# A hybrid decoder layer in float32: the MLP's down projection done one product at a time in all eight PSUM banks

## The chip, the cores and the metric

The kernel runs on one core of one Trainium2 chip. A core has a matrix engine (TensorE, PE in the profile), a vector engine (VectorE, DVE), an activation engine (ScalarE, ACT), a general engine (GpSimd, POOL) and a queue engine (SyncE, SP). Each works through its own queue of instructions in order. Data are moved between the chip's main memory and the on-chip memory SBUF by DMAs, which are issued from the queues of SP, ACT or POOL. Matrix products land in PSUM, which has eight banks; one bank holds a 128 x 512 float32 tile.

The metric is the time of one execution on the device in microseconds.

## The reference

One decoder layer over 2048 tokens of width 1024: a token mixer (a short gated convolution beside a Mamba-2 scan, each normalised, then one output projection) and a squared-ReLU MLP, both between two RMS norms. The change touches the MLP only:

```python
x = x + _rmsnorm(mix, norm_mix_post[i])
h = _rmsnorm(x, norm_mlp_pre[i])
f = jnp.square(jax.nn.relu(jnp.einsum("btd,df->btf", h, w_up[i])))   # d = 1024, f = 4096
f = jnp.einsum("btf,fd->btd", f, w_down[i])
x = x + _rmsnorm(f, norm_mlp_post[i])
```

## The kernel before, in words

**Precision.** A float32 product is made of three matmuls in a faster 32-bit type. Each operand is split into a high part (a cast on ACT, line 498) and a low part (a subtraction on DVE, line 499); then high x high, high x low and low x high go into the same PSUM bank (lines 695 to 697 and 751 to 753).

**Seven products for eight.** Both MLP projections use the Winograd form of Strassen's scheme. Each operand is cut into 2 x 2 blocks. Sums of blocks are made ahead (`left` at line 503 for the operand that PE loads as weights, `right_sums` at line 519 for the other), seven block products are formed in the order `ORDER = (0, 1, 5, 6, 4, 2, 3)`, and the four blocks of the result are sums of products. The 2048 tokens form two groups `g` of 1024, each of two blocks of 512; the 4096 hidden units form 16 pairs `p` of two 128-row tiles.

**Up stage** (lines 784 to 792). For each group, `hidden_blocks` (line 539) loads the 28 tiles of hidden block sums and splits them into 56 fixed buffers, named in `HOMES`. For each of 16 pairs, `up_weights` (line 667) loads four tiles of `w_up` into the ring `raw` (six buffers), makes four block sums on GpSimd, and splits seven tiles into the rings `wh` and `wl` (nine each). `up` (line 689) runs seven products of 12 matmuls each in the three banks tagged `mm`, adds them up on DVE (`plus`, line 702), squares the rectified blocks on ACT (lines 706 and 707) and stores the four finished blocks of the activations `f` to main memory from ACT's queue (line 708). On eight of the 16 pairs of each group, `down_weights` (line 676) also loads four tiles of `w_down` into `raw`, makes four block sums on GpSimd, splits seven tiles through the same rings `wh` and `wl`, and stores the 14 halves to main memory (line 687, SP's queue). `drain(1)` (line 553) also runs what is left over from the token mixer: the last output projection, norms, and the block sums of the hidden state (`hidden_sums`, line 527).

**Down stage** (lines 793 to 796). For each group, and for two pairs at a time, `f_load` (line 731) loads four tiles of `f` per pair, makes four block sums on GpSimd and splits seven tiles; `down_load` (line 722) loads the 14 stored halves of `w_down` per pair. Then for each product and each of four 128-token tiles, six matmuls go into one bank (the tags `ax` and `mm` in turn), and the bank is added to an SBUF accumulator (28 per group; a copy on ACT at line 756 for the first two pairs, an addition on DVE at line 758 for the others). With the last pairs, `combine` (line 762) makes the result blocks out of the seven accumulators on DVE and GpSimd, and `finish` (line 775) does the norm, the gain and the residual per 128 tokens: square and sum on ACT (line 115), two small operations on DVE (lines 117 and 109), a power on GpSimd (line 110), the gain (line 778), a load of `x1` on SP (line 780), a scale-and-add on DVE (line 781) and the store of the output on ACT's queue (line 782).

**What sets the order.** The code above is traced in the order written, and a scheduler then orders each engine's queue: among the instructions whose inputs and buffers are there by its own reckoning, the one written first goes first. So an engine's queue can leave the written order, and once it is fixed, each engine waits at the head of its queue.

Of the kernel before, what the change touches and what calls it, by code (L numbers as in the profile page):

```python
# [15 lines left out]
P = 128  # L16
# [23 lines left out]
    "us": 4, "uc": 7, "acc": 30, "fx": 2,  # L40
# [4 lines left out]
def hybrid_layer(ctx: ExitStack, tc: tile.TileContext, x, xT, w_in, w_dt, w_out, w_up, w_down,  # L45
# [413 lines left out]
    def mlp_input(m, tok):  # L459
        for i in range(2):  # L460
# [15 lines left out]
    f_d = [[[dram.tile([P, TB], F32, name=f"f{g}_{f}_{q}") for q in range(2)]  # L476
            for f in range(FF // P)] for g in range(NG)]
    dn_d = [[[dram.tile([P, 512], F32, name=f"dn{p}_{i}_{s}") for s in range(2)]
             for i in B7] for p in range(NP)]
# [13 lines left out]
    def ring(i):  # L493
        return "wh", "wl"

# [7 lines left out]
    def left(a11, a12, a21, a22, tags, eng):  # L503
        out = [None] * 7
        out[0] = split(a11, tags(0))
        out[1] = split(a12, tags(1))
# [3 lines left out]
        out[5] = split(s2, tags(5))  # L510
        eng.tensor_tensor(s3, a11, a21, op=ALU.subtract)
        out[6] = split(s3, tags(6))
        out[4] = split(s1, tags(4))
        eng.tensor_tensor(s4, a12, s2, op=ALU.subtract)
        out[2] = split(s4, tags(2))
        out[3] = split(a22, tags(3))
# [10 lines left out]
    def hidden_sums(g, k):  # L527
# [7 lines left out]
        blocks = right_sums(raw[0, 0], raw[0, 1], raw[1, 0], raw[1, 1], G)  # L535
# [131 lines left out]
    def up_weights(p):  # L667
        raw = {}
        for i in range(2):
            for j in range(2):  # L670
                raw[i, j] = big("raw")
                SY.dma_start(raw[i, j].rearrange("p (a b) -> p a b", a=4),
                             w_up[2 * p + i][:, 4 * j:4 * j + 4, :])
        return left(raw[0, 0], raw[0, 1], raw[1, 0], raw[1, 1], ring, G)

    def down_weights(p):
        raw = {}
        for j in range(2):
            for k in range(2):
                raw[j, k] = big("raw")  # L680
                SY.dma_start(raw[j, k].rearrange("p (a b) -> p a b", a=1),
                             w_down[2 * p + j][:, k:k + 1, :])
        blocks = right_sums(raw[0, 0], raw[0, 1], raw[1, 0], raw[1, 1], G)
        for i in ORDER:
            halves = split(blocks[i], ring(i))
            for s in range(2):
                SY.dma_start(dn_d[p][i][s], halves[s].bitcast(F32))

    def up(g, p, hb7, wb7):
        def product(i):  # L690
            pt = bank("mm")
# [13 lines left out]
        def store(c, i, q):  # L705
            S.activation(c, c, AF.Relu)  # L706
            S.square(c, c)
            S.dma_start(f_d[g][2 * p + i][q], c)
# [3 lines left out]
        store(plus(s1, product(1)), 0, 0)  # L712
# [4 lines left out]
        c22 = plus(u3, p5)  # L717
        store(c22, 1, 1)
        store(plus(u4, product(2)), 0, 1)
        store(plus(u3, product(3)), 1, 0)  # L720

    def down_load(p, m):
        out = [None] * 7
        for i in ORDER:
            hi, lo = (big(t, F32R) for t in home(i, 2 + m))
            SY.dma_start(hi.bitcast(F32), dn_d[p][i][0])
            SY.dma_start(lo.bitcast(F32), dn_d[p][i][1])
            out[i] = hi, lo
        return out

    def f_load(g, p, m):
        raw = {}
        for q in range(2):
            for j in range(2):
                raw[q, j] = big("raw")
                SY.dma_start(raw[q, j], f_d[g][2 * p + j][q])
        return left(raw[0, 0], raw[0, 1], raw[1, 0], raw[1, 1], lambda i: home(i, m), G)

    def down(ps_, g, acc, last):
        first = ps_[0] == 0  # L740
        fb = [f_load(g, p, m) for m, p in enumerate(ps_)]
        wb = [down_load(p, m) for m, p in enumerate(ps_)]
        todo = [(i, t) for i in ORDER for t in range(TT)]
        if last and g == NG - 1:
            todo.sort(key=lambda it: it[1])
        for n, (i, t) in enumerate(todo):
            ts = slice(t * P, (t + 1) * P)
            pt = bank(("ax", "mm")[n % 2])
            for m in range(len(ps_)):
                (fh, fl), (wh, wl) = fb[m][i], wb[m][i]  # L750
# [87 lines left out]
```

## Time and profile before

| | |
|---|---|
| median of 3 runs | 2823.98 us (2823.08 to 2827.82) |
| profiled execution | 2824.66 us; its span, first to last instruction, 2822.9 us |
| mean granted TensorE clock | 0.985 of full speed |
| busy share of the span | PE 97%, DVE 74%, ACT 48%, POOL 33% |
| moved by DMA | 536.61 MB, 190 GB/s over the span |
| first up matmul, first down matmul, last matmul start at | 1479.0, 2172.7, 2791.5 us |

Times are microseconds unless marked ns. In the lists of instructions in order of time, a row has the start, the duration, the engine, the line of the kernel, the operation and `out<-in` by tile names; in brackets stands how long the engine was idle before it and what released it. Rows of groups have a count, the busy time, the mean in ns of one, and the idle time before them with its releasers. Rows of waits have total, count and longest. A busy share in the 40 slices is in tenths (9 is 90% or more). Matmuls are pipelined: one starts before the one ahead of it has ended.

### The profile page before, as it was taken

What the parts mean: (1) busy time and instruction counts of PE and PEld (TensorE: products, weight loads), DVE (VectorE), ACT (ScalarE), POOL (GpSimd) and SP (SyncE); (2) the same over time, 40 slices, a digit from 0 to 9 for tenths busy, and PEclk for the clock granted to TensorE, in tenths of its full rate; (3) what the DMA queues carried; (4) which work ended last, traced back from release to release, by engine and by line L of the source; (5) the groups of instructions that cost most, each with busy time, mean ns of one, the idle gap of its engine ahead of it and who ended that gap; (6) DMA issues with size and microseconds to landing.
All of it is one profiled execution on the core that took longest, in us unless ns stands there. A gap on an engine that the chain in (4) does not pass through costs nothing. (4 is left out here: it accounts for less than half of the span.)

```text
span 2822.9 us, 38911 instructions
## 1 busy us (share of the span) xinstructions
PE 2725.5 (97%) x12822; PEld 2241.2 (79%) x12822; DVE 2086.8 (74%) x3511; ACT 1364.8 (48%) x2409; POOL 939.0 (33%) x682
## 2 busy tenths in 40 slices
PE   8999999999999999999999988799999999999995
PEld 6888888888888888788888767688888888878884
DVE  6675867767677668677586666697886688898888
ACT  6545535465355555454654555566666322252221
POOL 1120412123121225211133445544454233363324
PEclk9999999999999999999999999899999999999997
DMA  8323334432344336543344778777788877878773
GB/s 280 133 86 120 102 120 146 127 101 90 126 144 138 109 98 207 190 148 113 100 133 146 253 259 309 287 239 246 268 280 288 276 250 244 263 278 300 242 234 131
DMA packets 306426, 536.61 MB, mean 190 GB/s; under 512 B 32944, under 2 KB 49712, under 8 KB 306224
## 3 DMA queue, kind: packets, MB, share of 16 engines
q1 hardware_dynamic: 253328, 460.19, 49.1%
q10 hardware_dynamic: 52896, 73.94, 7.3%
q8 instruction: 101, 1.65, 0.2%
q14 instruction: 101, 0.83, 0.1%
HBM read 401.75 MB, written 132.25 MB: 189 GB/s over the span
## 5 line engine op out<-in xcount | busy, mean ns | idle before, releaser
L154 PE MATMUL mm<-hh,wh 128*128 128x512 f32 x1408 | 556.0, 395 | 4.4 <-DVE mix L444 2.3
L155 PE MATMUL mm<-hl,wh 128*128 128x512 f32 x1408 | 551.5, 392 | 0.5 <-DVE hl L144 0.5
L156 PE MATMUL mm<-hh,wl 128*128 128x512 f32 x1408 | 551.2, 392 | 0.0
L99 DVE TENSOR_TENSOR wl<-raw,wh 128x512 fp32r<-128x512 f32 x480 | 368.1, 778 | 236.2 <-ACT wh L98 225.8
L98 ACT CAST wh<-raw 128x512 fp32r<-128x512 f32 x480 | 293.0, 617 | 455.2 <-PE mm L155 297.8
L154 PEld LDWEIGHTS mm<-hh,wh 128*128 128x128 f32 x1408 | 266.1, 189 | 59.7 <-issue 3.5
L156 PEld LDWEIGHTS mm<-hh,wl 128*128 128x128 f32 x1408 | 265.8, 189 | 55.8
L155 PEld LDWEIGHTS mm<-hl,wh 128*128 128x128 f32 x1408 | 266.0, 189 | 54.9 <-DVE hl L144 1.2
L508 POOL TENSOR_TENSOR us<-raw 128x512 f32<-128x512 f32 x64 | 91.0, 1422 | 507.6 <-DMA raw<-w_up_dram 94.2
L499 DVE TENSOR_TENSOR wl<-us,wh 128x512 fp32r<-128x512 f32 x192 | 188.4, 999 | 73.8 <-ACT wh L498 59.2
L166 PE MATMUL ax<-wh,yh 128*128 128x512 f32 x512 | 201.3, 393 | 0.0
L168 PE MATMUL ax<-wh,yl 128*128 128x512 f32 x512 | 199.6, 390 | 0.0
L167 PE MATMUL ax<-wl,yh 128*128 128x512 f32 x512 | 199.4, 389 | 0.0
L702 DVE TENSOR_TENSOR uc<-uc,mm 128x512 f32<-128x512 f32 x224 | 149.4, 678 | 48.9 <-PE mm L697 35.1
L499 DVE TENSOR_TENSOR wl<-raw,wh 128x512 fp32r<-128x512 f32 x144 | 138.1, 966 | 38.6 <-ACT wh L498 24.9
L758 DVE TENSOR_TENSOR acc<-acc,ax 128x512 f32<-128x512 f32 x196 | 133.1, 679 | 44.6 <-PE ax L753 44.5
L706 ACT ACTIVATE uc<-uc 128x512 f32<-128x512 f32 x128 | 80.5, 629 | 153.1 <-DVE uc L702 137.7
L219 POOL TENSOR_TENSOR sq<-sq,v 128x512 f32<-128x512 f32 x28 | 37.2, 1327 | 351.8 <-ACT v L218 347.7
L110 POOL TENSOR_TENSOR cst<-cst 128x1 f32<-128x1 f32 (+1 forms) x76 | 60.7, 799 | 269.2 <-DVE cst L109 267.9
L758 DVE TENSOR_TENSOR acc<-acc,mm 128x512 f32<-128x512 f32 x196 | 133.0, 679 | 22.9 <-PE mm L753 22.2
L369 POOL TENSOR_TENSOR row<-row,cT 128x512 f32<-128x512 f32 x60 | 99.3, 1673 | 132.9 <-ACT cT L295 78.0
L498 ACT CAST wh<-us 128x512 fp32r<-128x512 f32 x192 | 113.4, 616 | 56.9 <-POOL us L509 29.9
(454 smaller groups left out, 6605.0 us busy)
## 6 DMA issues: line engine op xcount, KB each, us to landing
raw<-w_in_dram SPq DMA_DIRECT2D x352, 256.0 KB, 2.8
raw<-w_out_dram SPq DMA_DIRECT2D x128, 256.0 KB, 2.9
raw<-w_up_dram SPq DMA_DIRECT2D x128, 256.0 KB, 4.3
f<-uc ACTq DMA_DIRECT2D x128, 256.0 KB, 3.7
raw<-f SPq DMA_DIRECT2D x128, 256.0 KB, 4.2
dn<-wh SPq DMA_DIRECT2D x112, 256.0 KB, 4.1
dn<-wl SPq DMA_DIRECT2D x112, 256.0 KB, 4.1
row<-cs SPq DMA_DIRECT2D x64, 256.0 KB, 3.9
```

The source lines that it names most:

```text
L98: S.copy(hi, raw)
L99: V.tensor_sub(lo, raw, hi.bitcast(F32))
L154: PE.matmul(pt, lhsT=wh[:, ks], rhs=ah[k], start=(k == 0), stop=False)
L155: PE.matmul(pt, lhsT=wh[:, ks], rhs=al[k], start=False, stop=False)
L156: PE.matmul(pt, lhsT=wl[:, ks], rhs=ah[k], start=False, stop=(k == KT - 1))
L166: PE.matmul(pts[t], lhsT=a, rhs=wh, start=(i == 0), stop=False)
L167: PE.matmul(pts[t], lhsT=a, rhs=wl, start=False, stop=False)
L168: PE.matmul(pts[t], lhsT=c, rhs=wh, start=False, stop=(i == n - 1))
L498: S.copy(hi, v)
L499: V.tensor_sub(lo, v, hi.bitcast(F32))
L702: V.tensor_tensor(c, a, pt, op=ALU.add)
L758: V.tensor_tensor(acc[i, t], acc[i, t], pt, op=ALU.add)
```

## The change

The down stage is turned inside out. Instead of two pairs at a time over all products, it goes product by product: for each of the seven, all 16 pairs are summed inside PSUM, in eight banks at once, one for each 128-token tile of both groups (`sites`). Nothing is accumulated in SBUF over the pairs; when a product is whole, `close` copies or adds its bank into one of 32 running sums and, when a result block is complete (after products 1, 2 and 3), starts its norm and gain (`half`) and ends it (`finish`). In the last product the last six pairs are kept back (`LATE`) and done bank by bank instead of pair by pair.

The operands of the down stage are loaded unsplit and split on arrival (`down_operands`): per product and pair one tile of weights, shared by both groups, and one tile of activations per group. The block sums of the activations are made in the up stage (`summed`, on GpSimd) and stored from GpSimd's queue, those of `w_down` are made on DVE and stored unsplit, only where they are sums (`i > 2`). In the up stage the block sums of `w_up` move from GpSimd to DVE, as do the hidden block sums of the second group; the loads of `w_up` are issued one step earlier and alternate between `raw` and `yh`; the loads of `w_down` go into `yl`, ahead of the step's products; and the up products use the banks of both tags in turn. `finish` writes its first half from SP's queue and its second from ACT's. The core of the diff:

```diff
-    "us": 4, "uc": 7, "acc": 30, "fx": 2,
+    "us": 4, "uc": 10, "fs": 4, "acc": 32,
...
-        blocks = right_sums(raw[0, 0], raw[0, 1], raw[1, 0], raw[1, 1], G)
+        blocks = right_sums(raw[0, 0], raw[0, 1], raw[1, 0], raw[1, 1], V if g else G)
...
+    def up_load(g, p):
         raw = {}
         for i in range(2):
             for j in range(2):
-                raw[i, j] = big("raw")
+                raw[i, j] = big("yh" if p % 2 and (g or p > 2) else "raw")
                 SY.dma_start(raw[i, j].rearrange("p (a b) -> p a b", a=4),
                              w_up[2 * p + i][:, 4 * j:4 * j + 4, :])
-        return left(raw[0, 0], raw[0, 1], raw[1, 0], raw[1, 1], ring, G)
+        return raw
+
+    def up_weights(raw):
+        return left(raw[0, 0], raw[0, 1], raw[1, 0], raw[1, 1], V)
...
+    def down_sums(p, raw):
+        blocks = right_sums(raw[0, 0], raw[0, 1], raw[1, 0], raw[1, 1], V)
         for i in ORDER:
-            halves = split(blocks[i], ring(i))
-            for s in range(2):
-                SY.dma_start(dn_d[p][i][s], halves[s].bitcast(F32))
+            if i > 2:
+                SY.dma_start(dn_d[p][i], blocks[i])
...
-            pt = bank("mm")
+            pt = bank(("mm", "ax")[turn[0] % 2])
+            turn[0] += 1
...
+        def summed(i, a, b, op):
+            c = big("fs")
+            G.tensor_tensor(c, a, b, op=op)
+            save(i, c, G)
+            return c
...
+        a21 = relu2(plus(u4, product(2)))
+        t1 = summed(4, a21, a22, ALU.add)
+        t2 = summed(5, t1, a11, ALU.subtract)
+        summed(6, a11, a21, ALU.subtract)
+        a12 = relu2(plus(u3, product(3)))
+        save(1, a12, S)
+        summed(2, a12, t2, ALU.subtract)
...
+    def down_operands(i, p):
+        n = step[0]
+        step[0] += 1
+        raw = big("raw")
+        if i > 2:
+            SY.dma_start(raw, dn_d[p][i])
+        else:
+            SY.dma_start(raw.rearrange("p (a b) -> p a b", a=1),
+                         w_down[2 * p + (i > 0)][:, i // 2:i // 2 + 1, :])
+        w = split(raw, ("wh", "wl"))
+        f = []
+        for g in range(NG):
+            raw = big("xt")
+            SY.dma_start(raw, f_d[g][p][i])
+            f.append(split(raw, [r[n % len(r)] for r in ROUND[g]]))
+        return f, w
+
+    def half(m, s2, tok, i, eng):
+        S.activation(big("us"), m, AF.Square, accum_out=s2[:, i:i + 1])
+        eng.tensor_tensor(m, m, gmlp[i], op=ALU.mult)
+
+    def finish(m, s2, tok):
+        r = cols(1)
+        V.tensor_add(s2[:, 2:3], s2[:, 0:1], s2[:, 1:2])
+        rsqrt(r, s2[:, 2:3], D, s2[:, 0:1])
+        for i in range(2):
+            xt = big("uc")
+            SY.dma_start(xt, x1_d[tok][:, i * 512:(i + 1) * 512])
+            V.scalar_tensor_tensor(xt, m[i], r, xt, op0=ALU.mult, op1=ALU.add)
+            (SY, S)[i].dma_start(out[tok * P:(tok + 1) * P, i * 512:(i + 1) * 512], xt)
...
+        def close(i, k, pt):
...
+            elif i == 4:
+                u[k] = add(u[k], u[k], pt), add(None, w[k], pt)
+            elif i == 2:
+                add(u[k][0], u[k][0], pt)
+                half(u[k][0], s2[k], tok, 1, V)
+                finish([c[k], u[k][0]], s2[k], tok)
+                s2[k] = cols(3)
+                half(u[k][1], s2[k], tok + TT, 1, G)
+            else:
+                add(w[k], w[k], pt)
+                half(w[k], s2[k], tok + TT, 0, V)
+                finish([w[k], u[k][1]], s2[k], tok + TT)
+
         for i in ORDER:
...
+            late = LATE if i == ORDER[-1] else 0
+            banks = {k: bank("mm" if n < 3 else "ax") for n, k in enumerate(sites)}
...
+            kept = []
+            for p in range(NP):
+                ops = down_operands(i, p)
+                if p >= NP - late:
+                    kept.append((p, ops))
+                    continue
+                for k in sites:
+                    mac(p, ops, k)
+                    if p == NP - 1:
+                        close(i, k, banks[k])
+            for k in sites if kept else ():
+                for p, ops in kept:
+                    mac(p, ops, k)
+                close(i, k, banks[k])
...
+    raw = up_load(0, 0)
     for g in range(NG):
         hb7 = hidden_blocks(g)
         for p in range(NP):
-            wb7 = up_weights(p)
+            wb7 = up_weights(raw)
+            if (g, p) != (NG - 1, NP - 1):
+                raw = up_load(g + (p == NP - 1), (p + 1) % NP)
+            if due[g][p]:
+                dn = ahead.pop(0)
+                draw = down_sums_load(dn)
             up(g, p, hb7, wb7)
             drain(1)
...
+            if due[g][p]:
+                down_sums(dn, draw)
+    down_stage()
```

More of the change, by code (lines that the diff above doesn't have):

```diff
@@ L500, in split, with left @@
         return hi, lo
-    def left(a11, a12, a21, a22, tags, eng):
+    def left(a11, a12, a21, a22, eng):
+        ring = "wh", "wl"
         out = [None] * 7
-        out[0] = split(a11, tags(0))
-        out[1] = split(a12, tags(1))
+        out[0] = split(a11, ring)
+        out[1] = split(a12, ring)
         s1, s2, s3, s4 = (big("us") for _ in range(4))
@@ L716, in up @@
         u4 = plus(u2, p5)
[L717 to L723, printed above, removed]
-        for i in ORDER:
[L725 to L750, printed above, removed]
-                PE.matmul(pt, lhsT=fh[:, ts], rhs=wh, start=(m == 0), stop=False)
-                PE.matmul(pt, lhsT=fh[:, ts], rhs=wl, start=False, stop=False)
-                PE.matmul(pt, lhsT=fl[:, ts], rhs=wh, start=False, stop=(m == len(ps_) - 1))
-            if first:
-                acc[i, t] = big("acc")
-                S.copy(acc[i, t], pt)
-            else:
-                V.tensor_tensor(acc[i, t], acc[i, t], pt, op=ALU.add)
-            if last and i == ORDER[-1]:
-                combine(g, acc, t)
@@ L775, in finish @@
-    def finish(m, tok):
-        r = norm_scale(m, "fx")
-        for i in range(2):
-            (G, V)[i].tensor_tensor(m[i], m[i], gmlp[i], op=ALU.mult)
-            xt = big("fx")
-            SY.dma_start(xt, x1_d[tok][:, i * 512:(i + 1) * 512])
-            V.scalar_tensor_tensor(m[i], m[i], r, xt, op0=ALU.mult, op1=ALU.add)
-            S.dma_start(out[tok * P:(tok + 1) * P, i * 512:(i + 1) * 512], m[i])
+        a22 = relu2(plus(u3, p5))
+        save(3, a22, S)
+        a21 = relu2(plus(u4, product(2)))
@@ new lines, in up @@
+        t1 = summed(4, a21, a22, ALU.add)
[4 more added lines that the diff above has]
+        summed(2, a12, t2, ALU.subtract)
+    LATE = 6
+    ROUND = (HOMES[0], HOMES[2]), (HOMES[1], HOMES[3])
+    step = [0]
+    def down_operands(i, p):
[14 more added lines that the diff above has]
+        return f, w
@@ L784, in hybrid_layer @@
     ahead = list(range(NP))
+    due = [[p in at for p in range(NP)] for at in
+           ((3, 5, 7, 9, 11, 13, 15), (3, 4, 6, 7, 8, 10, 11, 12, 14))]
+    raw = up_load(0, 0)
     for g in range(NG):
@@ L787, in hybrid_layer @@
         for p in range(NP):
-            wb7 = up_weights(p)
+            wb7 = up_weights(raw)
[4 more added lines that the diff above has]
+                draw = down_sums_load(dn)
             up(g, p, hb7, wb7)
             drain(1)
-            if 2 < p < NP - 2 and p % 3 != 2:
-                down_weights(ahead.pop(0))
-    for g in range(NG):
-        acc = {}
-        for p in range(0, NP, 2):
-            down((p, p + 1), g, acc, p + 2 == NP)
+            if due[g][p]:
+                down_sums(dn, draw)
+    down_stage()
 def kernel(x, norm_mix_pre, w_in, conv_a_w, ssm_conv_w, ssm_conv_b, dt_bias, a_log, d_skip,
```

75 lines of the change are left out of this document (45 added, 30 removed).

## The prediction

> **What bounds the kernel now.** I read the page first, for the busy line of TensorE (PE) over the span and the clock it was granted.
>
> ```profile
> span 2822.9 us, 38911 instructions
> PE 2725.5 (97%) x12822; PEld 2241.2 (79%) x12822; DVE 2086.8 (74%) x3511; ACT 1364.8 (48%) x2409; POOL 939.0 (33%) x682
> ...
> PE   8999999999999999999999988799999999999995
> ...
> PEclk9999999999999999999999999899999999999997
> ```
>
> PE is the bound nearly everywhere; the weak slices are 23 to 26 (from about 1600 us) and the last. The change removes no matmul, so it can only win PE's idle time. How much there is needs the price of one matmul, from the list of PE's instructions in order of time: the first and the last of 20 neighbours at the end of the down stage.
>
> ```profile
> 2787.23 0.39 PE L752 MATMUL ax<-xdl,bT 128*128 128x512 f32 x1
> ...
> 2791.54 0.39 PE L753 MATMUL mm<-dts,z 128*128 128x512 f32 x1
> ```
>
> They start 4.31 us apart, 19 steps: 0.227 us a matmul (the 0.39 is pipelined). So three cost 0.68, eighteen 4.08, twenty-four 5.44, an up step of 84 19.05. Next, the windows: up stage until PE is last starved, the rest of it, the down stage, and what follows PE's last matmul.
>
> ```profile
> core 0: us, PE busy (x) PEld busy (x) DVE busy (x) ACT busy (x) POOL busy (x), PEclk, DMA share, GB/s
> 1478.50:1905.00 426.50, 387.28 (x1646) 312.02 (x1646) 300.32 (x397) 243.55 (x449) 204.03 (x142) 0.95 0.72 249
> 1905.00:2172.70 267.70, 267.70 (x1182) 221.72 (x1181) 213.38 (x261) 163.65 (x291) 133.33 (x87) 1.00 0.75 265
> 2172.70:2792.10 619.40, 612.66 (x2689) 505.18 (x2687) 505.56 (x683) 167.50 (x318) 232.69 (x164) 1.00 0.77 257
> 2792.10:2822.90 30.80, 0.00 (x0) 0.00 (x0) 24.94 (x34) 5.05 (x14) 15.20 (x13) 0.53 0.23 85
> ```
>
> *Up* lasts 694.2 us. It holds 2688 up matmuls and 96 of the last output projection (2784 x 0.2268 = 631.4) and 32 transposes (about 5): 57.5 us are lost, all before 1905, where the clock is 0.95 too. *Down* lasts 619.4 for 2688 x 0.2268 = 609.7: only 9.7 lost. The *tail* without PE is 30.8. So 98 us are within reach. Who starves PE is told by the waits of its weight loads between 1478.5 and 1905 (total, times, longest).
>
> ```profile
> PEld mm L695 <- ACT wh L498: 25.8, 11, 7.9
> PEld mm L697 <- DVE wl L499: 18.4, 12, 5.2
> PEld ax L463 <- ACT mix L457: 5.4, 2, 3.9
> PEld mm L696 <- DVE wdt L499: 1.0, 1, 1.0
> ```
>
> The same view for all engines, 1500 to 1900, tells what stands ahead of those splits.
>
> ```profile
> POOL us L508 <- DMA raw<-w_up_dram: 65.7, 7, 19.5
> ...
> ACT wh L498 <- POOL us L509: 29.3, 8, 7.0
> ```
>
> 44.2 of 50.6 us are waits for split weights; the splits wait for POOL's block sums, those for w_up loads. Why the loads are late shows in SP's instructions in order of time around the longest case, and in the largest of SP's waits, 1480 to 2170.
>
> ```profile
> 1742.40 0.53 SPq L672 DMA_DIRECT2D raw<-w_up_dram  x1
> 1743.02 0.64 SPq L533 DMA_DIRECT2D xt<-h  x1
> 1743.78 1.26 SPq L672 DMA_DIRECT2D raw<-w_up_dram  x2
> 1746.19 0.33 SPq L687 DMA_DIRECT2D dn<-wh  x1
> 1748.25 0.33 SPq L672 DMA_DIRECT2D raw<-w_up_dram  x1
> ```
> ```profile
> SPq L687 <- ACT wh L498: 91.7, 53, 7.5
> ```
>
> Loads and the stores of split down weights (L687) alternate, and the stores hold SP until their cast is done.
>
> **The up stage, edit by edit.** *Removed:* the seven splits (ACT cast, DVE subtraction) of each of 16 w_down pairs, 160 of 224 dn stores on SP, and POOL's sums of w_up (128 in 32 steps), of w_down (64) and of the second group's hidden blocks (16). *Added:* those 208 sums on DVE, and per step four POOL sums and seven f stores in place of four, four of them issued by POOL. *Moved:* w_up loads one step earlier, into two sets of buffers, so that on SP they stand ahead of the step's w_down loads and dn stores; the w_down loads go ahead of the up products, their sums stay behind. The products turn over eight PSUM banks instead of three. Prices, from the groups of 1905 to 2172.7:
>
> ```profile
> L499 DVE TENSOR_TENSOR wl<-us,wh 128x512 fp32r<-128x512 f32 x84 | 86.3, 1046 | 14.2 <-ACT wh L498 14.2
> L702 DVE TENSOR_TENSOR uc<-uc,mm 128x512 f32<-128x512 f32 x99 | 66.6, 680 | 31.7 <-PE mm L697 31.3
> ...
> L508 POOL TENSOR_TENSOR us<-raw 128x512 f32<-128x512 f32 x14 | 19.1, 1368 | 86.4 <-DMA raw<-w_up_dram 28.5 <-DVE wl L499 21.2 <-PE mm L697 19.8
> ```
>
> A DVE operation with one operand in PSUM (L702) is 0.68, with both in SBUF (L499) 1.05: beside POOL the second kind stretches. DVE was busy 213.4 of 267.7 us, 15.2 per step of 19.05. Per step it had 7 splits and 7 additions, and 7 more splits on half the steps: 17.5; at 0.60 from start to start (rows of the tail below) 10.5. The other 4.7 us over six POOL operations is 0.78 each. Afterwards: 7 + 7 + 4 + 4/2 = 20 operations, 12.0 us, and four POOL sums, 3.1: 15.1, so DVE's load stays (the 16 hidden sums add 10 us in the first 427, where it is busy for 300). POOL's four sums at 1.37 to 1.7 and their stores fit 19 us as long as a store costs POOL under 3; nothing in this stage reads them.
>
> The Trainium skill (SBUF — State Buffer, "Who interferes with whom") has a DVE instruction with two SBUF inputs fully blocked while a GpSimd instruction that reads SBUF runs, which speaks against DVE sums beside POOL sums. By that full lock the four would cost 4 x 1.37 = 5.5 rather than 3.1, 17.5 us a step: still under 19.05, and L499 against L702 agrees in kind.
>
> So the loads come a step early, no cast holds SP, and a left sum costs 0.60 instead of 1.4. Upper end of the gain G: the 44.2 us and the slow clock that goes with them (57.5 - 50.6 = 6.9), 51. Lower end: the one stall quoted, where PE lost about 8. I take 45, near the top because every large wait hangs on the edited chain; what is late next is the transposes' wait (5.4) and the second group's hidden blocks.
>
> **The down stage.** Removed: 448 dn loads, 128 f loads, 128 POOL sums, 392 accumulations. Added: per product and pair, three loads and three splits, 336 of each, and 56 additions. DVE then does 1.8 us per 5.44 us step (it was busy 505 of 619) and ACT's casts are as many: all of it lies under PE, eight steps of buffers ahead. DMA falls from 576 loads to 336; of the 32 out stores 16 go from ACT's queue to SP's, which now has three loads a step. What is new is the hand-over between products: all eight banks are full, and bank k is wanted again 4.76 us after its last matmul. One copy or addition per bank (0.60) keeps up with PE (0.68); two additions in product 4 run 0.4 us late. After product 2 each bank also brings a closing: addition, gain multiply, two small operations, a POOL power, two scale-and-add, and one POOL multiply. The rows for that are the last closing of before, from several engines' lists; the first two show what POOL does to such operations.
>
> ```profile
> 2808.50 1.75 DVE L769 TENSOR_TENSOR acc<-acc 128x512 f32<-128x512 f32 x1
> ...
> 2811.84 0.68 DVE L768 TENSOR_TENSOR acc<-acc 128x512 f32<-128x512 f32 x1
> ...
> 2816.08 0.63 ACT L115 ACTIVATE fx<-acc 128x512 f32<-128x512 f32 x1 [2.96 <-DVE acc L781]
> ...
> 2816.83 0.16 DVE L117 TENSOR_TENSOR cst<-cst 128x1 f32<-128x1 f32 x1 [0.51 <-ACT fx L115]
> 2816.91 0.68 DVE L778 TENSOR_TENSOR acc<-acc,gain 128x512 f32<-128x512 f32 x1
> 2817.51 0.15 DVE L109 TENSOR_SCALAR cst<-cst 128x1 f32<-128x1 f32 x1
> ...
> 2817.74 0.55 POOL L110 TENSOR_TENSOR cst<-cst 128x1 f32<-128x1 f32 x1 [2.62 <-DVE cst L109]
> ...
> 2818.32 1.41 DVE L781 SCALAR_TENSOR_TENSOR acc<-acc,cst,fx 128x512 f32<-128x512 f32 x2 [0.66 <-POOL cst L110]
> ```
>
> Let s be DVE's time per closing. Its own work is 4 x 0.60 + 2 x 0.08 = 2.6; one lock by POOL adds 1.75 - 0.68 = 1.0: s = 3.6. The last bank's addition is then done 7s + 1 after the first bank filled and wanted after 4.76 + 7 x 0.68 = 9.5; PE waits 7s - 8.5 = 16.7 us. With 2 for the start and the other hand-overs, down loses 18.7 where it lost 9.7: +9.0.
>
> **The tail.** The last six pairs of product 3 go bank by bank, so a bank closes every 4.08 us, slower than s, and only the last closing follows PE: addition 0.69, then the quoted chain from 2816.08 to the span's end at 2822.9 (6.8) less the 0.60 that L109 stood behind L778: 7 us. 30.8 becomes 7: -23.8. Without that order of the last six pairs, eight closings would follow PE, 8 x 3.6 - 4.8 + 7 = 31, no gain.
>
> **The sum.** The profiled execution took 2824.66 (span 2822.9), 0.7 above the median 2823.98. 2824.66 - 45 + 9.0 - 23.8 = 2764.9.
>
> **Rivals.** *A: the up loads stay late.* If the stall is DMA bandwidth (share 0.72 to 1905) and the rest of stage one, not queue order, G is about a third, 15: 2794.9. Against it: the second half shows 0.75 and not one PE wait. *B, the other side: closings run in the order written.* SP's store of a token's first half stands ahead of the load of its second half of x1; if SP keeps that order, every closing waits for a whole load.
>
> ```profile
> fx<-x SPq DMA_DIRECT2D x32, 256.0 KB, 4.4
> ```
>
> Then s = 0.68 (addition) + 0.75 (square, to L117) + 0.31 (L117 and L109) + 0.58 (power) + 0.70 + 0.33 (issue) + 4.4 + 0.70 = 8.5: PE waits 7 x 8.5 - 8.5 = 51 after product 2 (+43.3 in all), and the tail becomes 8 x 8.5 - 32.6 + 7 = 42.4 (+11.6): 2824.66 - 45 + 43.3 + 11.6 = 2834.6. It decides above s = 7.8, where 15s - 117.6 (the sum of those three terms) is nil. Against it, DVE's queue already leaves the written order: an accumulation runs inside a combine.
>
> ```profile
> 2758.69 0.69 DVE L765 TENSOR_TENSOR acc<-acc 128x512 f32<-128x512 f32 x1
> 2759.33 0.69 DVE L758 TENSOR_TENSOR acc<-acc,mm 128x512 f32<-128x512 f32 x1
> 2760.05 1.29 DVE L766 TENSOR_TENSOR acc<-acc 128x512 f32<-128x512 f32 x1
> ```
>
> The load needs only a free buffer (ten), so I expect it early. *C: POOL's own DMA issues block DVE.* No row shows one. If each of four takes d from DVE, a step costs 15.1 + 4d and passes PE at d = 1.0; with d = 1.75, the longest blocked row, it is 22.1, up takes 32 x 22.1 + 27 = 734, 40 longer: 2824.66 + 40 + 9 - 23.8 = 2850. At d = 0, the other end, nothing; I take 0 to 1, since POOL's sums themselves cost 0.78.
>
> The Trainium skill (DMA: Bandwidth & Descriptors, "Latency and other measured facts") gives about 1 us to the first byte on the path from GpSimd, whose cores write the descriptors; as an estimate 15.1 + 4 = 19.1, on the edge. No run here shows it yet.
>
> *D: more is won.* G = 57 and s = 2.6: 2824.66 - 57 + 2 - 23.8 = 2746.
>
> **How the numbers follow.** Forecast 0.58 (own range 2750 to 2782), A 0.18, B 0.10, D 0.06, C 0.05, the rest 0.03 near no change. The time is 2765. A range of 2744 to 2802 holds forecast, A and D, 0.82. A measurement of this kernel tells about 0.2%, 5.6 us: faster 0.85 (forecast, A, D, a mild B), same 0.03, slower 0.12.
>
> **What would show it.** Right: waits of PE's weight loads in the up stage under 12 us, its clock near 1.0; one PE gap of 10 to 20 us where product 2 hands over to 3, put down to DVE additions; PE's last matmul within 10 us of the end. Wrong: w_up loads still ahead of PE's waits (A); SP out stores ahead of x1 loads and a closing near 8.5 us (B); DVE over 95% busy in the up stage with POOL solid (C).

## The result, and the profile after

The changed kernel takes 2867.4 us (median of 4 runs, 2865.1 to 2868.6) against 2824.5 for the kernel before on the same chip: 1.0149 times as long (95% interval 1.0132 to 1.0167). The forecast was 2765, a gain; it went the other way by 43 us. Two of the three terms of the sum came out near their size (the one for the down stage by luck, as shown further down). The third, the up stage, which should have given 45 us, took 53. In two of the experiments below (fewer buffers, four places taken) one execution took 4472.9 and 3893.6 us, at granted clocks of 0.569 and 0.655; their medians are those of the other executions.

The page of the changed kernel, busy lines and slices:

```profile
span 2865.2 us, 37725 instructions
PE 2747.2 (96%) x12822; PEld 2247.6 (78%) x12822; DVE 1879.9 (66%) x3351; ACT 1351.6 (47%) x2361; POOL 646.8 (23%) x578
...
PE   8999999999999999999999989889989999999998
```

The weak slices are still in the up stage, and now they lie between the 24th and the 30th of the 40 (before, between the 24th and the 26th). The windows, cut as before: the up stage up to 1905, the rest of it to the first down matmul (2226.78), the down stage, the tail.

```profile
core 0: us, PE busy (x) PEld busy (x) DVE busy (x) ACT busy (x) POOL busy (x), PEclk, DMA share, GB/s
1478.50:1905.00 426.50, 373.35 (x1560) 298.00 (x1559) 304.17 (x432) 212.28 (x377) 141.18 (x145) 0.94 0.67 226
1905.00:2226.78 321.78, 300.93 (x1275) 241.88 (x1273) 231.44 (x311) 145.60 (x248) 115.53 (x120) 0.97 0.56 191
2226.78:2854.96 628.18, 616.40 (x2689) 507.49 (x2687) 298.37 (x461) 211.41 (x402) 42.70 (x38) 0.99 0.50 161
2854.96:2865.20 10.24, 0.00 (x0) 0.00 (x0) 4.76 (x11) 0.72 (x2) 1.10 (x2) 0.72 0.27 102
```

From the first up matmul (1480.3) the up stage now lasts 746.5 us, 52.8 more than before; the second window, in which PE had not waited at all, is hit as well. Down is 9.0 longer, the tail 20.7 shorter (each stage taken from the start of its first matmul, the tail from the start of PE's last), and the first up matmul is 1.3 later: before rounding +42.3, the difference of the spans. DVE is busy 72% of the up stage and POOL 34%: neither is full. The waits of PE's weight loads (total, times, longest), 1480 to 2230:

```profile
PEld mm L703 <- DVE wl L496: 43.0, 22, 5.5
PEld mm L701 <- ACT wh L495: 23.2, 11, 6.5
PEld ax L703 <- DVE wl L496: 15.6, 13, 2.5
PEld ax L701 <- ACT wh L495: 11.3, 5, 4.6
```

These are 93 us of waits for split weights where there were 44. Before, the splits waited for block sums on POOL and those for the loads of `w_up`. The longest waits of the splits in the changed kernel, and all that any engine waited for loads of `w_up` and `w_down`, in the same stretch:

```profile
ACT wh L495 <- POOL fs L721: 59.0, 32, 4.8
DVE wl L496 <- POOL fs L721: 45.4, 18, 5.8
...
POOL f L717 <- DMA yl<-w_down_dram: 0.3, 1, 0.3
POOL f L717 <- DMA yh<-w_up_dram: 0.3, 1, 0.3
POOL f L717 <- DMA raw<-w_up_dram: 0.3, 1, 0.3
```

So the loads are on time, as meant: 0.9 us of waits. But the splits of *weights* now wait for POOL's sums of *activations* (`fs`, line 721), which they do not read. One such stretch, from the lists in order of time (start, duration, and in brackets the idle time before and what ended it), POOL, then ACT, DVE and PE:

```profile
2015.46 1.29 POOL L721 TENSOR_TENSOR fs<-uc 128x512 f32<-128x512 f32 x1 [10.24 <-ACT uc L713]
2017.05 0.56 POOL L717 DMA_DIRECT2D f<-fs  x1 [0.30 <-POOL fs L721]
2017.63 1.30 POOL L721 TENSOR_TENSOR fs<-fs,uc 128x512 f32<-128x512 f32 x1
2018.88 1.28 POOL L721 TENSOR_TENSOR fs<-uc 128x512 f32<-128x512 f32 x1
2020.11 1.09 POOL L717 DMA_DIRECT2D f<-fs  x2
2021.63 1.71 POOL L721 TENSOR_TENSOR fs<-uc,fs 128x512 f32<-128x512 f32 x1 [0.43 <-ACT wh L495]
2023.63 0.56 POOL L717 DMA_DIRECT2D f<-fs  x1 [0.30 <-POOL fs L721]
...
2023.37 0.62 ACT L495 CAST wh<-raw 128x512 fp32r<-128x512 f32 x1 [1.31 <-POOL fs L721]
2025.48 0.62 ACT L495 CAST wh<-yh 128x512 fp32r<-128x512 f32 x1 [1.01 <-DMA f<-fs]
...
2020.20 0.69 DVE L512 TENSOR_TENSOR us<-raw,us 128x512 f32<-128x512 f32 x1 [2.72 <-POOL fs L721]
...
2024.81 0.80 PE L703 MATMUL mm<-xdt,wl 128*128 128x512 f32 x1 [2.48 <-DVE wl L496]
```

POOL stands idle for 10 us of a step and then runs one chain of 8.7 us: sum, 0.30 of waiting, 0.56 of issuing its store, next sum. Meanwhile a cast of a *loaded* tile waits for POOL, the next one for a store of `fs` to land, and a weight sum on DVE waits 2.7 us for POOL. The inputs of all three come from loads or from DVE. What they wait for is the memory that they are to write. The built program shows how that can be: every 128 x 512 tile lies in one of 100 places of 2 KB, and tiles of all tags share them. A tag's number in `BUFS` only limits how many tiles of it are alive together. Where few places are free, a new tile gets one just left by a tile of another engine, and its first write waits for that engine's last read, or for the DMA that still reads it. Counted in the built programs over the up stage (how many matmuls stand, in the scheduled order, between the last use of a place and its next use by a split weight; how many load tiles and split weights are alive on average):

```
                               matmuls between,     loads   split weights
                               median for wh / wl   alive   alive
before                              25 / 24           4.9      13.6
changed                              3 / 3           19.5       8.5
```

At 0.227 us a matmul the reuse distance fell from 5.6 us to 0.7. And POOL is often the engine that had the place: in the built program of the change 105 of 475 split weights of the up stage take a place that POOL used last, 53 after an activation that its sums read and 52 after a sum.

### The profile page after: what moved, and what is told of

Same layout as the page of the kernel before. It is cut to its first block, busy times and chain, and to the rows that moved or that the text cites. A ratio compares the mean times of both kernels' runs of the same rounds, so it can differ in the third digit from the quotient of the medians.

```text
span 2865.2 us, 37725 instructions
## 1 busy us (share of the span) xinstructions
PE 2747.2 (96%) x12822; PEld 2247.6 (78%) x12822; DVE 1879.9 (66%) x3351; ACT 1351.6 (47%) x2361; POOL 646.8 (23%) x578
## 5 line engine op out<-in xcount | busy, mean ns | idle before, releaser
L99 DVE TENSOR_TENSOR wl<-raw,wh 128x512 fp32r<-128x512 f32 x480 | 369.0, 779 | 236.7 <-ACT wh L98 228.0
L98 ACT CAST wh<-raw 128x512 fp32r<-128x512 f32 x480 | 293.0, 617 | 461.3 <-PE mm L155 292.8
L496 DVE TENSOR_TENSOR wl<-raw,wh 128x512 fp32r<-128x512 f32 x163 | 118.9, 733 | 106.2 <-ACT wh L495 57.7
L822 PE MATMUL ax<-wh,hl 128*128 128x512 f32 x448 | 176.0, 394 | 8.1 <-DVE acc L785 6.5
L721 POOL TENSOR_TENSOR fs<-uc 128x512 f32<-128x512 f32 x64 | 87.0, 1359 | 416.7 <-ACT uc L713 250.4
L823 PE MATMUL ax<-wl,hl 128*128 128x512 f32 x448 | 175.7, 392 | 0.0
L496 DVE TENSOR_TENSOR wl<-us,wh 128x512 fp32r<-128x512 f32 x128 | 116.2, 916 | 84.9 <-POOL fs L721 38.8
L495 ACT CAST wh<-raw 128x512 fp32r<-128x512 f32 x163 | 100.2, 618 | 146.0 <-PE ax L824 68.2
L495 ACT CAST hl<-xt 128x512 fp32r<-128x512 f32 x120 | 74.3, 620 | 145.1 <-PE ax L823 102.9
L495 ACT CAST wh<-us 128x512 fp32r<-128x512 f32 x128 | 76.7, 617 | 129.0 <-POOL fs L721 36.8
L767 POOL TENSOR_TENSOR acc<-acc,gain 128x512 f32<-128x512 f32 x16 | 24.5, 1553 | 500.2 <-PE ax L824 338.4
L822 PE MATMUL mm<-wh,hh 128*128 128x512 f32 x336 | 131.3, 391 | 1.1 <-DVE uc L708 1.1
```

The source lines that it names most:

```text
L98: S.copy(hi, raw)
L99: V.tensor_sub(lo, raw, hi.bitcast(F32))
L495: S.copy(hi, v)
L496: V.tensor_sub(lo, v, hi.bitcast(F32))
L822: PE.matmul(banks[k], lhsT=fh[:, ts], rhs=wh, start=(p == 0), stop=False)
L823: PE.matmul(banks[k], lhsT=fh[:, ts], rhs=wl, start=False, stop=False)
```

## The experiments

Three theories. T1: the rings of loads (6, 8 and 8 tiles) and the other new buffers crowd the places. T2: POOL's chain, with its own stores, holds tiles too long. T3: the order on DVE, where the weight sums now stand behind additions that wait for PE. All medians below come with their difference from the kernel before on the same chip, since that moved between 2821.9 and 2824.2; the change itself is +42.8. Where no interval is given it is 0.1% to 0.2% of the time to either side.

**Fewer buffers.**

```diff
-    "dtk": 1, "raw": 6, "wh": 9, "wl": 9, "hh": 8, "hl": 8, "xt": 6, "xtok": 2,
+    "dtk": 1, "raw": 8, "wh": 9, "wl": 9, "hh": 8, "hl": 8, "xt": 6, "xtok": 2,
...
-    "us": 4, "uc": 10, "fs": 4, "acc": 32,
+    "us": 4, "uc": 7, "fs": 2, "acc": 32,
...
-                raw[i, j] = big("yh" if p % 2 and (g or p > 2) else "raw")
+                raw[i, j] = big("raw")
...
-                raw[j, k] = big("yl")
+                raw[j, k] = big("raw")
```

> Only numbers of buffers change: uc 10 to 7, fs 4 to 2, and all loads of the up stage from one ring of 8, so that the tiles of the up stage fit the hundred places of 2 KB that all tiles share (56 hidden halves + 8 + 18 + 4 + 7 + 2 + 2 = 97; with the change as made 116). Theory T1 (too many buffers for the places, so that a weight waits for a place): 2800 to 2820, the up stage back at about 700 us. Theory T2 (POOL's chain of sums and its own stores holds the tiles that a weight's place was): 2857 to 2880, as the change made it, the waits of the splits for POOL's fs still there. Theory T3 (order: DVE's weight sums stand behind the additions that wait for TensorE): 2857 to 2880 too.

Measured 2821.6, -0.4: 43 us better than the change. T1, though by 2 us above its range.

**The sums of the activations on DVE, their stores from SP.**

```diff
-            G.tensor_tensor(c, a, b, op=op)
-            save(i, c, G)
+            V.tensor_tensor(c, a, b, op=op)
+            save(i, c, SY)
```

> The four sums of the activations' blocks on DVE instead of POOL, their stores from SP instead of POOL; POOL is empty in the up stage. Theory T2 (POOL's chain holds the places): 2795 to 2820, the up stage's loss of 115 us falls to 50 to 70, since a sum on DVE takes about 0.6 us against 1.3 plus 0.9 of waiting and issuing on POOL. Theory T1 (too many buffers): within 10 us of 2867. Theory T3 (order on DVE): 2867 to 2895, DVE gets 2.4 us more in every step and more stands ahead of the weight sums.

Measured 2805.2, -16.8: 60 better. T2; and DVE with four more operations a step is not the bound, so T3 falls.

**The same, and the weight sums back on POOL** (`up_weights` with `G` in place of `V`).

> The weight sums back on POOL, as before the change, and the sums of the activations' blocks on DVE with their stores from SP. Theory T3 (order on DVE): 2800 to 2825, since the weight sums no longer stand in DVE's order. Theory T2 (POOL's chain after the activations holds the places): 2795 to 2825 too, this run doesn't part these two, but with the run that has both on DVE it does: if that run stays slow and this one is fast it is the order, if both are fast it is POOL's chain. Theory T1 (too many buffers): within 10 us of 2867. A lock between DVE and POOL: within 15 us of 2867, since POOL still makes four sums in each step.

Measured 2798.9, -23.0. POOL makes as many sums as in the change, and the time is 66 lower: it matters which sums stand there, or who issues their stores. This run changes both; a later one parts them.

**No sums of activations.**

> Leaves out the four sums of the activations' blocks; the block a21 is stored in place of the first of them, and the down stage reads a stored block for each sum that it would read, so its work is the same. Theory T2: 2790 to 2815, the whole loss over before goes. A lock between DVE and POOL: the same. Theory T1 (four buffers of 116 fewer, still over a hundred): 2840 to 2867. Theory T3 (order on DVE, where the weight sums remain): 2845 to 2867.

Measured 2771.8, -50.1, below every range. All that the up stage lost hangs on these four sums and their stores (of the four stores of a step, one is kept for `a21`).

T1 and T2 both stand; either alone gives 43 to 60 us, of about 100. The next runs part them.

**Only the stores from SP, the sums on POOL** (`save(i, c, SY)`).

> The sums of the activations' blocks stay on POOL, only their stores are issued by SP. The first four runs left two causes standing together: too many buffers for the hundred places (fewer buffers: 2821.8) and POOL's chain (sums on DVE: 2805.2). Here the chain loses the issue and the idle time around it, 0.56 + 0.30 of some 2.2 us for each sum, and keeps the sums at 1.29. If it is POOL's own stores that make the chain long: 2825 to 2845. If it is the sums on POOL themselves: 2855 to 2870. If a store on SP holds up the loads behind it: above 2875.

Measured 2821.5, -0.6: 43 better, more than its range, from nothing but the queue that issues 128 stores.

**Both cuts: sums on DVE, stores from SP, 97 buffers.**

> The sums of the activations' blocks on DVE with stores from SP, and the buffers cut to 97 as in the run with fewer buffers. If the two causes are separate, their gains add for a good part: 2765 to 2785. If both are one cause (a place held by POOL's chain), what is left after the one is little moved by the other: 2795 to 2810. If DVE with 24 sums and splits in a step is the bound by now: not under 2795 either, but with waits for DVE's own work instead of waits for stores.

Measured 2766.4, -55.6 (ratio 0.9798, 0.9782 to 0.9814): the gains add. This is the fastest kernel of the study and beats both. Its page and its windows (up, down, tail):

```profile
span 2769.6 us, 37538 instructions
PE 2713.8 (98%) x12822; PEld 2238.2 (81%) x12822; DVE 1879.1 (68%) x3479; ACT 1350.9 (49%) x2361; POOL 398.8 (14%) x322
```
```profile
1485.06:2140.46 655.40, 640.41 (x2826) 527.89 (x2824) 541.09 (x876) 361.30 (x637) 19.41 (x17) 0.99 0.72 244
2140.46:2759.40 618.94, 612.48 (x2689) 506.68 (x2687) 289.26 (x450) 206.45 (x390) 33.99 (x30) 0.99 0.48 159
2759.40:2769.60 10.20, 0.00 (x0) 0.00 (x0) 4.80 (x11) 0.72 (x2) 1.08 (x2) 0.76 0.28 103
```

The up stage is 38.3 shorter than before and the clock in it 0.99.

**Weight sums on POOL with 97 buffers.**

> The weight sums on POOL as before the change, the sums of the activations' blocks on DVE with stores from SP, and the buffers cut to 97. If the two causes are separate: 2755 to 2780. If they are one: 2790 to 2805.

Measured 2781.4, -40.7, 1 us above the range for separate causes. With room in SBUF it is better to leave POOL empty than to give it the weight sums.

**Only `uc` and `fs` cut.**

> Only uc goes from 10 to 7 and fs from 4 to 2; the loads keep their buffers as the change made them, so 111 tiles are allowed for a hundred places. If the number over a hundred is what counts: 2845 to 2862, less than half of the 45 us that the cut to 97 gave. If it is the activations' tiles, which POOL's chain holds: 2815 to 2830, nearly all of the 45. If it was the loads' rings alone: 2860 to 2872.

Measured 2871.8, +49.7: nothing gained. Adding up limits, as I had done (116 for 100 places), says little: of ten `uc` allowed, 2.5 are alive on average.

**Only the loads' rings cut.**

> Of the cut to 97 buffers only the loads' part: all loads of the up stage from one ring of 8 instead of rings of 6, 8 and 8; uc stays at 10, fs at 4. Cutting uc and fs alone gave nothing (2871.8). If the places that loads hold early are the cause: 2812 to 2830, as with the whole cut (2821.8). If cutting uc and fs and cutting the loads work only together: 2845 to 2870.

Measured 2825.2, +1.0: the whole gain of the cut comes from the loads.

**Sums on POOL, stores from SP, 97 buffers.**

> The sums stay on POOL, their stores go to SP, and the buffers are cut to 97: the run with sums on DVE and the cut (2766.4) with the sums put back on POOL. If only POOL's own stores and the loads' places cost time: 2762 to 2778. If the sums on POOL cost something of their own (longer than DVE's, or a lock with DVE): 2785 to 2815. If the two cuts have one cause: 2800 to 2820, hardly under either alone (2821.5, 2821.8).

Measured 2782.9, -41.4, between its first two ranges. With this run the prices can be read as steps between pairs of runs that differ in one thing (the lower row also has the smaller `uc` and `fs`, which gave nothing by themselves):

```
                                        sums on POOL,   sums on POOL,   sums on DVE,
                                        POOL stores     SP stores       SP stores
difference from before, three rings        +42.8           -0.6           -16.8
difference from before, one ring           -0.4           -41.4           -55.6
```

The loads' rings cost 43, 41 and 39 us; POOL's own stores 43 and 41; sums on POOL rather than on DVE 16 and 14. The three hardly touch each other. Not all of it is lost in the up stage: with one ring the down stage takes 633.0 us with POOL's stores, 623.5 with stores from SP and 618.6 with the sums on DVE, since its first matmuls wait for the last additions of the up stage. What remains is why.

**Taken places.** In the fastest kernel, eight, four and then ten tiles are written ahead of the up stage and read after it:

```diff
+    dead = [big("dead") for _ in range(8)]
+    for d in dead:
+        G.memset(d, 0.0)
...
+    for d in dead:
+        V.tensor_add(d[:, 0:1], d[:, 0:1], a12[:, 0:1])
     down_stage()
```

> The run with sums on DVE and 97 buffers (2766.4), and eight tiles more that are written once ahead of the up stage and read after its last step: eight of the hundred places are taken and nothing else is changed, no load, no sum, no store. If the number of free places is the cause by itself: 2790 to 2815, about what the loads' rings cost with the sums on DVE (2805.2), the waits for split weights back. If the loads' rings cost time in another way (earlier loads that crowd the queues): 2764 to 2775.

> The same with four tiles taken instead of eight. If free places are the cause, between the two: 2770 to 2795. If they are not: 2764 to 2773.

> The run with sums on DVE and 97 buffers (2766.4) with ten places taken through the up stage. In the built program a place is then written again 3 to 4 matmuls (median) after its last use, as in the run with sums on DVE and the loads' three rings (2805.2; 4 to 6), against 11 without the taken places. If the quick reuse of places is the cause: 2785 to 2810. If the loads' rings cost time by the loads themselves: under 2782.

Measured 2779.4, 2776.3 and 2794.2 (-44.8, -48.0, -28.8): 11, 8 and 27 us worse than without; eight places fell between both ranges, four and ten into those for places as the cause. So taken places alone, with no load changed in the code, bring back 27 of the 39 us that three rings cost. They bring back the waits for the low parts too, though not those for the high parts (16.2 us in the fastest kernel, 10.9 with ten taken places). PE's weight loads, two rows of the fastest kernel, then three with ten taken places:

```profile
PEld mm L703 <- DVE wl L496: 1.1, 1, 1.1
PEld ax L703 <- DVE wl L496: 1.0, 2, 0.7
```
```profile
PEld mm L703 <- DVE wl L496: 13.5, 6, 4.7
PEld mm L701 <- ACT wh L495: 7.1, 5, 3.8
PEld ax L703 <- DVE wl L496: 5.6, 5, 2.1
```

The other 12 us were not parted: with twelve places taken the tiles no longer fit. Nor is one rival out: in the built program the taken places also put the queues of DVE and ACT into another order, so the wait for a place is not parted from an order that the scheduler chose because places were few.

**Few weights ahead, but free places.** A crowd has two effects: fewer split weights stand ready, and places are reused at once. Here the first without the second:

```diff
-        ring = "wh", "wl"
+        ring = "vh", "vl"
...
+    "gain": 2, "vh": 4, "vl": 4,
```

> The same kernel, the up stage's split weights limited to 4 high and 4 low parts instead of 9 and 9, no place taken: 7.0 stand ready on average instead of 14.7, and a place is written again 28 matmuls after its last use. If the number of weights that stand ready is the cause: 2795 to 2820. If it is the quick reuse of places: 2764 to 2778.

Measured 2769.7, -53.3, 2 us from the fastest. Seven weights ahead suffice; what costs is that places are few and reused at once. The counts beside the times, all with sums on DVE and stores from SP:

```
                          matmuls between, wh / wl   split weights alive   difference
97 buffers                       11 / 11                   14.7              -55.6
  weights limited to 4 + 4       28 / 28                    7.0              -53.3
  4 places taken                  5 / 6                    13.4              -48.0
  8 places taken                  5 / 5                    11.1              -44.8
  10 places taken                 4 / 3                     9.7              -28.8
three rings of loads              4 / 6                     7.9              -16.8
```

The distance is not the whole measure. Counted in the same way, the kernel with fewer buffers and POOL's stores has 10 / 9, and those stores still cost it 41 us; there POOL had the place last for 90 of 473 split weights, in the fastest kernel for none.

**POOL's stores without POOL's sums** (sums on DVE, `save(i, c, G)`, 97 buffers).

> Sums on DVE, 97 buffers, and their stores issued by POOL, which does nothing else in the stage. If a store that POOL issues costs by itself (it lands later, holds its tile longer, or its issue holds up DVE): 2790 to 2812. If it costs only because POOL's next sum stands behind it: 2762 to 2775.

Measured 2777.1, -45.9: 10 us worse than from SP, between my two cases. **A second, small store behind each sum**, the real one from SP:

```diff
+            d = dram.tile([P, 64], F32, name=f"dd{g}_{p}_{i}")
+            G.dma_start(d, c[:, :64])
```

> Sums on POOL, their stores from SP, 97 buffers (2782.9), and behind each sum a second small store by POOL (128x64 of the sum, to a place that nobody reads). If the place of the issue in the queue of POOL's sums is what costs: 2810 to 2830, as with the real stores on POOL (2821.8). If it is the real store's landing: 2780 to 2792.

Measured 2823.1, 0.0: 41 us worse than without it, as much as the real stores cost. POOL's groups of stores, first with sums on DVE, then with the small stores:

```profile
L717 POOL DMA_DIRECT2D f<-fs x128 | 70.0, 547 | 563.2 <-DVE fs L721 556.1 <-issue 3.7 <-DMA h<-eph 3.2
```
```profile
L724 POOL DMA_DIRECT2D dd<-fs x128 | 71.8, 561 | 39.8 <-POOL fs L721 34.0 <-issue 2.9 <-DMA f<-uc 1.5
```

An issue takes POOL 0.55 to 0.56 us in both, for 256 KB as for 32 KB. Where POOL also makes the sums, each store waits for its sum (34.0 over 128, 0.3 each), and the next sum stands behind it. The landing is no dearer by itself: with sums on DVE and 97 buffers its median was 3.3 us from POOL and 3.3 from SP. With stores from SP the chain is short; POOL's list of one step with sums on POOL, stores from SP and 97 buffers:

```profile
2006.22 1.29 POOL L721 TENSOR_TENSOR fs<-uc 128x512 f32<-128x512 f32 x1 [13.29 <-ACT uc L713]
2007.59 1.62 POOL L721 TENSOR_TENSOR fs<-fs,uc 128x512 f32<-128x512 f32 x1
2009.18 1.28 POOL L721 TENSOR_TENSOR fs<-uc 128x512 f32<-128x512 f32 x1
2010.43 1.73 POOL L721 TENSOR_TENSOR fs<-uc,fs 128x512 f32<-128x512 f32 x1
```

5.9 us instead of 8.7, and the activations that the sums read are let go that much sooner. The small store also reads the sum, so the sum's place is free only when it has landed: with it the low parts waited 42.5 us for `dd<-fs` to land, without it 25.3 us for `f<-fs`. So the run shows what a store costs that POOL issues among its sums, whatever its size; it does not part the issue's place in the queue from the later landing behind it. A changed order is no rival here: in the built programs PE's queue is the same with POOL's stores, with SP's and with the small ones, and DVE's nearly so.

**Whether reuse still costs in the fastest kernel** (loads' ring 7, split weights 7 + 7 in rings of their own).

> The run with sums on DVE and 97 buffers (2766.4) with the loads' ring at 7 instead of 8 and the up stage's split weights at 7 and 7 in rings of their own: a place is written again 21 to 28 matmuls (median) after its last use instead of 9 to 12. If quick reuse still costs there: 2750 to 2762. If 11 matmuls were enough: 2763 to 2770. If fewer loads and weights ahead now come late: above 2772.

Measured 2769.9, -53.7: with the sums on DVE a distance of 11 matmuls was enough.

**The tail without the late order** (`LATE = 0`).

> The run with sums on DVE and 97 buffers (2766.4) without the last part of the change: the eight sums of product 3 are finished product step by product step like the others, so that all eight closings come in the last step. The wait at the hand-over from product 2 to 3 in the changed kernel, 6.5 us where 16.7 were forecast, gives 2.1 us for each closing (7s - 8.5 = 6.5); then the tail goes from 10 to about 8 x 2.1 - 8 x 0.68 + 7 = 18, the time to 2772 to 2777. By the 3.6 us of the forecast it would be 30, 2784 to 2790. If the order of the last product is worth nothing: 2764 to 2768.

Measured 2782.5, -41.1: 14.5 worse than with it. The window after PE's last matmul:

```profile
2757.20:2780.70 23.50, 0.00 (x0) 0.00 (x0) 18.00 (x39) 3.53 (x10) 4.55 (x7) 0.61 0.78 279
```

23.5 us instead of 10.2, between both expectations: 8s - 4.8 + 7 = 23.5 gives s = 2.7. (DVE's own list says 3.1; see the tail below.)

## Why the prediction was wrong

**The failing step** is in the paragraph on the up stage: "POOL's four sums at 1.37 to 1.7 and their stores fit 19 us as long as a store costs POOL under 3; nothing in this stage reads them." The durations were right (1.3 to 1.7, and 0.86 with the wait), and so is the last clause. What it missed is that something in this stage *writes where they read*. I had costed POOL's sums by POOL's time and by DVE's lock, not by the tiles that they hold. Measured: their stores in the sums' queue 41 to 43 us, the sums on POOL rather than DVE 14 to 16 (how much of these is DVE's lock was not parted).

**The second omission** is in "*Moved:* w_up loads one step earlier, into two sets of buffers". I counted only the gain. The loads did come in time (waits for them 0.9 us), but 19.5 tiles of loads alive instead of 4.9 took places from the splits: 39 to 43 us. A place that is written 0.7 us after its last use was nowhere in my sum, since I read a tag's number as buffers of its own.

**G = 45** was near the right size for what it meant. With both causes out, the up stage is 38.3 shorter than before, inside the bounds 8 to 51. The forecast of 2765 stands 1 us from that kernel's 2766.4 (as differences, -59.8 and -55.6), partly by luck in the smaller terms: there the first up matmul comes 6 us late, down is 0.3 shorter where 9.0 longer was forecast, and the tail gives 20.8, not 23.8.

**Down, +9.0.** In the changed kernel down is indeed 9.0 longer, but not as worked out; that the number fits is luck. One PE gap at the hand-over from product 2 to 3, put down to DVE additions, was there as said:

```profile
2772.91 0.79 PE L822 MATMUL ax<-wh,hl 128*128 128x512 f32 x1 [6.52 <-DVE acc L785]
```

It is 6.5 us, not 16.7. By 7s - 8.5 that would make s 2.1, but DVE's list shows closings that take longer than my 3.6, in another order; rows of DVE, then one of POOL:

```profile
2754.73 1.88 DVE L785 TENSOR_TENSOR acc<-acc,mm 128x512 f32<-128x512 f32 x3
2756.52 0.68 DVE L785 TENSOR_TENSOR acc<-acc,ax 128x512 f32<-128x512 f32 x1
...
2758.90 0.68 DVE L785 TENSOR_TENSOR acc<-acc,ax 128x512 f32<-128x512 f32 x1
...
2760.70 3.48 DVE L776 SCALAR_TENSOR_TENSOR uc<-acc,cst,uc 128x512 f32<-128x512 f32 x2 [0.46 <-POOL cst L110]
...
2772.17 0.68 DVE L785 TENSOR_TENSOR acc<-acc,ax 128x512 f32<-128x512 f32 x1
...
2787.99 1.41 DVE L776 SCALAR_TENSOR_TENSOR uc<-acc,cst,uc 128x512 f32<-128x512 f32 x2 [0.44 <-POOL cst L110]
```
```profile
2760.64 4.69 POOL L767 TENSOR_TENSOR acc<-acc,gain 128x512 f32<-128x512 f32 x3
```

The eight closings take DVE from 2754.73 to 2789.4, with two splits among them: 4.2 us each. The lock is there: beside POOL's multiplies two scale-and-adds take 3.48 us, elsewhere 1.41. What failed is "The last bank's addition is then done 7s + 1 after the first bank filled": the additions do not stand one closing apart. Five of the eight run ahead of the first scale-and-add, and PE waits for the sixth alone. The rest of the loss in down stands right behind the gap, where about ten matmuls start 0.43 us apart instead of 0.23, and at the stage's start, where the last up steps are late (this part is gone in the fastest kernel).

**The tail, -23.8.** Measured -20.7 from the start of PE's last matmul; in the window behind it 10.2 us remain where I had 7. DVE's list after PE's last matmul (which starts at 2854.57) shows the 3 us:

```profile
2856.08 1.41 DVE L776 SCALAR_TENSOR_TENSOR uc<-acc,cst,uc 128x512 f32<-128x512 f32 x2 [0.66 <-POOL cst L110]
2857.41 0.68 DVE L785 TENSOR_TENSOR acc<-acc,ax 128x512 f32<-128x512 f32 x1
```

The last addition starts 2.8 us after the last matmul, behind the closing before it. A bank does close every 4.08 us, but a closing takes longer than that from end to end, so two overlap. The late order itself is worth 13.3 us of tail (23.5 less 10.2), not the 24 of my text. In the run without it DVE's eight closings go from 2752.48 to 2777.47, 3.1 us each and not 3.6, since those of product 3 have no POOL multiply beside them; and my 7 us behind the eight held the last closing a second time.

**The rivals.** A (loads stay late) is out by the 0.9 us of waits. B (closings in the written order, s = 8.5) is out: five additions ran ahead, and a closing took 4.2 and 3.1 us. C named the right instructions, POOL's own stores, and a price near theirs (40 us), for a wrong reason: it had them block DVE until DVE is full, and DVE is busy 72%. DVE's low-part subtractions show it, sums on DVE and 97 buffers, first with stores from SP, then from POOL:

```profile
L496 DVE TENSOR_TENSOR wl<-us,wh 128x512 fp32r<-128x512 f32 x124 | 84.8, 691 | 18.5 <-ACT wh L495 13.7 <-PE ax L167 1.3 <-DMA f<-uc 1.0
```
```profile
L496 DVE TENSOR_TENSOR wl<-us,wh 128x512 fp32r<-128x512 f32 x124 | 86.3, 704 | 23.1 <-ACT wh L495 14.3 <-DMA hs<-xt 3.8 <-DMA f<-fs 2.8
```

691 against 704 ns: beside issues alone DVE is not held up. Beside POOL's *sums* it is (one ring, stores from SP):

```profile
L496 DVE TENSOR_TENSOR wl<-us,wh 128x512 fp32r<-128x512 f32 x124 | 101.9, 831 | 45.1 <-DMA f<-fs 25.3 <-ACT wh L495 14.1 <-POOL fs L721 4.0
```

831 ns, 0.14 more. The Trainium skill (SBUF — State Buffer, "Who interferes with whom") says the same of the kind: a DVE instruction with two SBUF inputs contends with a GpSimd instruction that reads SBUF. Over seven splits it is 1 us a step, and over all of DVE's operations with two SBUF inputs in that list about 2, less than the 3.1 us that I had put on DVE for POOL's four sums. The rule of the Trainium skill that I cited for rival C (DMA: Bandwidth & Descriptors, "Latency and other measured facts": a later first byte from GpSimd than from SP or ACT) isn't what decided: 3.3 us to landing from either queue in that pair of runs. (Over all runs the medians are 2.8 to 3.4 from POOL, 2.1 to 3.8 from SP; the lowest is that of sums on POOL and stores from SP, and no run parts the first byte from the rest.) Of the 41 us that POOL's stores cost, 10 are there without POOL's sums too; the other 31 come only where a store stands ahead of the next sum.

**Still open.** How 2.8 us more of POOL's chain become 1.3 us (41 / 32) of each step was not followed instruction by instruction; it goes through places too, since the splits' waits name `fs`. Nor were the last 12 of the 39 us for the loads' rings parted, nor, in the other 27, the wait for a place from the changed order of the queues.

## What to carry to other kernels

An edit that adds tiles, or lets them live longer, can have a price even if nobody on the path reads them: when tags share SBUF, ask who writes next where the tile lay, and count in the built order how soon, and behind which engine. A wait on an engine that produces none of an instruction's inputs is the sign of it in a profile. And work on a side engine is costed not by whether it fits that engine's time, but by how long its chain, with the stores that it issues itself, keeps its inputs.

## What had not been expected of the hardware

A store issued by POOL holds POOL's own queue for 0.55 to 0.56 us and waits 0.3 us for the sum ahead of it, for 32 KB as for 256 KB, and landed no later than one from SP in the pair of runs that differ in nothing else (3.3 us each). Between SP and POOL as the issuer of the same 128 stores lay 41 to 43 us of the kernel's time where POOL made the sums, and 10 where it did not.
